# A residual convolution: the first image pair is stored from ACT's queue, beside the last loads of SyncE's queue

## Chip, cores, metric

One core of one Trainium2 chip. Times are device microseconds of one execution, as the median of several runs. A "span" is the time from the first to the last instruction in the records of a run; it leaves out a part at the end (1.83 us in the profiled run of the kernel before: 123.0 us against a span of 121.17 us). In the profile lines PE is TensorE (PEld its weight loads), DVE is VectorE, ACT is ScalarE, POOL is GpSimd and SP is SyncE; q1 is the DMA queue that SyncE fills, q10 the one that ACT fills.

## The reference

```python
x:        (16, 64, 64, 64) float32
weight:   (64, 64, 3, 3)   float32
residual: (16, 64, 64, 64) float32
# 3x3 convolution, padding 1, summed over input channels, then
return (output + residual).astype(np.float32)
```

## The kernel before

The images are handled in pairs. A pair of x, of residual or of output is one tile of 128 partitions x 4096 floats, 2.097 MB. SyncE's queue issues all loads and then all stores; only one half of the first x pair comes from ACT's queue. ACT casts x to bf16, TensorE does six accumulating matmul passes per image, VectorE adds the result to the residual in place (tile `ro`), and `ro` is stored.

```python
def load_ro(p):
    nc.sync.dma_start(out=ro[p][:, :], in_=res_bc[128*p : 128*p+128, :]).then_inc(s_r[p], 16)

def store(p):
    return nc.sync.dma_start(out=out_bc[128*p : 128*p+128, :], in_=ro[p][:, :])

# SyncE
for p in range(NPAIR):                       # NPAIR = 8, NXR = 3 buffers for x
    if p >= NXR:
        nc.sync.wait_ge(s_half, 2 * (p - NXR) + 3)
    ...                                      # p == 0: first half of x, and the weights
    else:
        load_x(p)
    load_ro(p)
for p in range(NEARLY):                      # NEARLY = 6
    nc.sync.wait_ge(s_add, 2 * p + 3)
    store(p).then_inc(s_out, 16)

# ACT
for n in range(B):                           # 16 images
    if im == 0:
        nc.scalar.wait_ge(s_x[p % NXR], ...)
    ... two casts ...

# after all engines have met
for p in range(NEARLY, NPAIR):
    store(p)                                 # SyncE, the last two pairs
```

## Time and profile before

| | before |
|---|---|
| time, median of the first 3 runs | 123.16 us (123.14 to 123.23) |
| bytes moved | 50.48 MB |
| last addition ends | 104.1 us |
| last store issued | 104.8 us |
| last store landed | 120.2 us |

The page divides the span into 40 slices of 3.03 us. Its row "DMA" is the busy share of the 16 DMA engines in tenths, and the row "GB/s" under it is what they moved. A transfer issued by an engine's sequencer waits in that engine's queue; the row of the sequencer (SPq, ACTq) shows the issue alone, not the movement. The Trainium skill says so too ("Perfetto Trace Analysis", section "DMA Instruction — HWDGE (DVE, Sync)"), and the trace agrees: issues take 0.33 to 0.58 us, and stores land 11 to 35 us later.

### The profile page before, as it was taken

The numbers are of one execution on the slowest core, as the hardware profiler recorded it, in microseconds if no ns is written. First come the engines' busy times: TensorE is split into PE (matmuls) and PEld (weight loads), VectorE is DVE, ScalarE is ACT, GpSimd is POOL, SyncE is SP. The second block draws the span as 40 slices with busy tenths as digits, with TensorE's granted clock in tenths as the row PEclk, the third lists the DMA queues.
The fourth block names the chain that finished last, engine by engine and source line by source line (L and its number), as shares of the span: only waits on it lengthen the run. The fifth ranks groups of instructions, "written<-read, shape, count | busy, mean of one in ns | idle before, by whom it ended". The sixth has DMA issues, their size and how long they took to land.

```text
span 121.2 us, 736 instructions
## 1 busy us (share of the span) xinstructions
PE 87.7 (72%) x389; PEld 10.7 (9%) x105; DVE 76.0 (63%) x40; ACT 63.1 (52%) x37; POOL 2.4 (2%) x16
## 2 busy tenths in 40 slices
PE   0033499999999999999999999999999980000000
PEld 0021001101010101010101010101010100000000
DVE  0005300889898898989889898898989889300000
ACT  4049969938966984993993994896000000000000
POOL 5200000000000000000000000000000000000000
PEclk9999999999999999999999999999999999755555
DMA  6999999999999999999999999999999999999993
GB/s 168 427 444 433 433 433 433 433 427 433 433 427 427 433 433 427 427 433 427 433 433 433 433 433 422 433 389 433 433 433 433 422 433 433 433 433 433 427 433 151
DMA packets 3744, 50.48 MB, mean 417 GB/s; under 512 B 416, under 2 KB 544, under 8 KB 544
## 3 DMA queue, kind: packets, MB, share of 16 engines
q1 hardware_dynamic: 3600, 49.43, 96.3%
q10 hardware_dynamic: 144, 1.05, 2.0%
HBM read 33.70 MB, written 16.78 MB: 417 GB/s over the span
## 4 chain that ended last, share of the span: by engine, by line
PE 71%; DVEq 2%; DVE 2%; issue 0%
PE ps L86 53%; PE ps L85 17%; DVEq L129 2%; DVE ro L201 2%
## 5 line engine op out<-in xcount | busy, mean ns | idle before, releaser
L201 DVE TENSOR_TENSOR ro<-ps,ro 64x2048 f32<-64x2048 f32 x32 | 73.2, 2289 | 17.7 <-PE ps L86 17.2
L86 PE MATMUL ps<-xp,wl 128*128 128x504 bf16 (+1 forms) x288 | 80.0, 388 | 0.2
L173 ACT CAST xp<-xr 64x2048 bf16<-64x2048 f32 x16 | 30.3, 1896 | 19.3 <-DMA xr<-in_x_dram 17.1
L85 PE MATMUL ps<-xp,wl 128*128 128x504 bf16 (+1 forms) x92 | 35.8, 389 | 3.4 <-PEq L222 3.4
L177 ACT CAST xp<-xr 64x2048 bf16<-64x2048 f32 x16 | 30.4, 1897 | 0.4
L85 PEld LDWEIGHTS ps<-xp,wl 128*128 128x128 bf16 x96 | 9.5, 99 | 79.1 <-issue 79.1
L189 DVE CAST wl<-ps 32x192 bf16<-32x192 f32 x8 | 2.8, 348 | 10.4 <-PE ps L214 10.3
L214 PE MATMUL ps<-ident,wraw 128*32 128x128 f32 x9 | 2.1, 412 | 8.1 <-DMA wraw<-in_weight_dram 8.1
L214 PEld LDWEIGHTS ps<-ident,wraw 128*32 128x32 f32 x9 | 1.2, 137 | 8.6 <-issue 8.1
L173 ACT ACT_TABLE_LOAD x1 | 1.3, 1283 | 1.1 <-SPq L129 1.1
L182 ACT CAST wl<-ps 32x192 bf16<-32x192 f32 x4 | 1.2, 306 | 0.0
L160 POOL MEMSET xp<- 64x64 bf16 x4 | 0.6, 147 | 0.2
L159 POOL MEMSET xp<- 64x64 bf16 x4 | 0.6, 145 | 0.2
L148 POOL TENSOR_SCALAR_AFFINE_SELECT ident<-ident 128x128 f32<-128x128 f32 x1 | 0.3, 295 | 0.2 <-POOL ident L146 0.2
L162 POOL MEMSET wl<- 64x192 bf16 x1 | 0.3, 253 | 0.1
L161 POOL MEMSET wl<- 64x192 bf16 x1 | 0.3, 252 | 0.1
L146 POOL MEMSET ident<- 128x128 f32 x1 | 0.2, 205 | 0.7 <-SPq L129 0.7
L257 POOL MEMSET const-uint8-127<- 128x1 uint8 x1 | 0.1, 113 | 0.0
L257 POOL MEMSET const-bfloat16-1.0<- 128x1 bf16 x1 | 0.1, 112 | 0.0
L257 POOL MEMSET const-float32-1.0<- 128x1 f32 x1 | 0.1, 109 | 0.0
L257 POOL MEMSET const-float32-0.0<- 128x1 f32 x1 | 0.1, 104 | 0.2 <-issue 0.2
## 6 DMA issues: line engine op xcount, KB each, us to landing
ro<-in_residual_dram SPq DMA_DIRECT2D x8, 2048.0 KB, 21.9
out_dram<-ro SPq DMA_DIRECT2D x8, 2048.0 KB, 28.2
xr<-in_x_dram SPq DMA_DIRECT2D x7, 2048.0 KB, 17.5
xr<-in_x_dram SPq DMA_DIRECT2D x1, 1024.0 KB, 7.0
xr<-in_x_dram ACTq DMA_DIRECT2D x1, 1024.0 KB, 7.6
wraw<-in_weight_dram SPq DMA_DIRECT2D x1, 144.0 KB, 6.9
```

Of the source, the lines that this page charges most:

```text
L85: return e.matmul(out=out_, lhsT=lhsT, rhs=rhs, start=start, stop=stop, skip_group_check=True)
L86: return e.add_instruction(mybir.InstMatmult(name=nc.get_next_instruction_name(), engine=PE, ins=[e.lower_ap(rhs), e.lower_ap(lhsT)], outs ...
L129: with tc.tile_critical(no_gpsimd_drain=True):
L159: nc.gpsimd.memset(t[0:64, 0, :], 0.0).then_inc(s_id, 1)
L160: nc.gpsimd.memset(t[64:128, J, :], 0.0).then_inc(s_id, 1)
L173: i = nc.scalar.copy(out=t[64:128, 0:J, :], in_=x4[hp, :, 0, :])
L177: nc.scalar.copy(out=t[0:64, 1 : J + 1, :], in_=x4[hp, :, 1, :]).then_inc(s_pack, 1)
L182: i = nc.scalar.copy(**weight_block(h, *b))
L189: i = nc.vector.tensor_copy(**weight_block(h, *b))
L201: i = nc.vector.tensor_tensor(out=o4[hp, :, par, :], in0=psj[64 * par : 64 * par + 64, :, :], in1=o4[hp, :, par, :], op=ADD)
L214: i = nc.tensor.transpose(out=tp[0:32, t // 3, 128 * (t % 3) : 128 * (t % 3) + 128], in_=wraw3[:, :, t], identity=ident[:, :])
L257: nc = _bacc.Bacc("TRN2", target_bir_lowering=False, num_devices=1)
```

## The change

The intent: store 0 should no longer wait for all loads to be through SyncE's queue. ACT issues it while the last loads are under way.

```diff
-    def store(p):
-        return nc.sync.dma_start(out=out_bc[128 * p : 128 * p + 128, :], in_=ro[p][:, :])
+    def store(p, engine=nc.sync):
+        return engine.dma_start(out=out_bc[128 * p : 128 * p + 128, :], in_=ro[p][:, :])
...
-        for p in range(NEARLY):
+        for p in range(1, NEARLY):
             nc.sync.wait_ge(s_add, 2 * p + 3)
             store(p).then_inc(s_out, 16)
... in ACT's loop over the images, after the casts:
+            if n == 12:
+                nc.scalar.wait_ge(s_add, 3)
+                store(0, nc.scalar).then_inc(s_out, 16)
```

## The prediction

> **What bounds the kernel now.** First the page, for which resource is busy in every slice.
>
> ```profile
> PE   0033499999999999999999999999999980000000
> ...
> DMA  6999999999999999999999999999999999999993
> ...
> DMA packets 3744, 50.48 MB, mean 417 GB/s; under 512 B 416, under 2 KB 544, under 8 KB 544
> ...
> q1 hardware_dynamic: 3600, 49.43, 96.3%
> q10 hardware_dynamic: 144, 1.05, 2.0%
> ```
>
> The DMA row has a 9 in 38 of its 40 slices, while PE begins in the third slice and is done seven slices (21 us) before the end. SyncE's queue q1 and ACT's queue q10 together hold the 16 DMA engines for 98.3% of the span. The chain of waits gives PE 71%, but it follows the compute to 104.1 us and does not account for the stores that drain after it, so I don't take it for the bound. The bound is 50.48 MB through engines that are never idle.
>
> Second, the DMA view of a stretch with loads alone (44 to 76 us) and of one with stores alone (84 to 116 us):
>
> ```profile
> DMA packets 957, 13.84 MB, mean 433 GB/s; under 512 B 112, under 2 KB 112, under 8 KB 112
> ```
> ```profile
> DMA packets 956, 13.83 MB, mean 432 GB/s; under 512 B 112, under 2 KB 112, under 8 KB 112
> ```
>
> Both directions run at the same rate to 0.3%. A pair of images is 128 x 4096 x 4 B = 2.097 MB, so one pair-sized transfer takes 2.097 MB / 433 GB/s = 4.84 us.
>
> Third, the border between loads and stores, in windows one slice wide (the last two columns are the DMA share and GB/s):
>
> ```profile
> 75.75:78.78 3.03, 3.03 (x15) 0.39 (x4) 2.42 (x3) 2.50 (x2) 0.00 (x0) 1.00 1.09 427
> 78.78:81.81 3.03, 3.03 (x16) 0.30 (x4) 3.00 (x2) 3.00 (x2) 0.00 (x0) 1.00 0.95 395
> 81.81:84.84 3.03, 3.03 (x16) 0.39 (x4) 2.46 (x2) 2.09 (x2) 0.00 (x0) 1.00 1.00 427
> ```
>
> The border costs (433 - 395) / 433 x 3.03 us = 0.27 us. That is all there is to win at it.
>
> Fourth, the timeline of ACT, for when the moved store is issued and how long ACT can be late:
>
> ```profile
> 68.45 1.90 ACT L177 CAST xp<-xr 64x2048 bf16<-64x2048 f32 x1
> 70.37 1.90 ACT L173 CAST xp<-xr 64x2048 bf16<-64x2048 f32 x1
> 72.29 1.90 ACT L177 CAST xp<-xr 64x2048 bf16<-64x2048 f32 x1
> 76.26 1.90 ACT L173 CAST xp<-xr 64x2048 bf16<-64x2048 f32 x1 [2.08 <-DMA xr<-in_x_dram]
> ```
>
> The casts of image 12 end at 70.35 us; the last x load (pair 7) has landed at 76.2 us. From the tile views of residual and output, by issue and landing: the last residual load, issued at 59.1 us, lands 22.2 us later (81.3); store 0, issued at 59.6, lands 26.6 later (86.2); store 5, issued at 86.3, lands 24.2 later (110.5); stores 6 and 7 are issued at 104.4 and 104.8 and land at 115.3 and 120.2. Spaced 4.9 us apart, they leave no hole.
>
> **What the Trainium skill says.** The page "DMA: Bandwidth & Descriptors", section "Issuing engines are not separate DMA queues", says that transfers from different issuing engines "will ultimately run on the same 16 DMA engines and interleave" and that spreading them saves only sequencer time. The trace agrees as far as it can: in the second and third slices, where the halves of the first x pair were in flight from SyncE and ACT, the page has 427 and 444 GB/s, the same as with one queue. Its section "Queues, rings and completion order" has each engine take turns between its queues, one packet at a time. No stretch of this trace has a load and a store in flight from two queues, so what alternating directions cost is not shown. Its section "Where 436 GB/s comes from" gives 435 GB/s as the ceiling of the SBUF ports; the measured 433 and 432 are at it.
>
> **The change part by part.**
> 1. Removed from SyncE: one wait and one issue (0.38 us median in the tile view of the output). The wait for the first pair's additions (over at about 34.4 us, when the first addition of image 2 ends) has long been satisfied at 59.6 us, and SyncE then waits for VectorE anyway (24.9 us in four waits before store issues). Gain: 0.
> 2. Added on ACT: one issue after image 12's casts, some 0.4 us. ACT idles 2.08 us before image 14, so it costs 0.
> 3. Moved: 2.097 MB, from behind the last residual load to beside the last two loads. Bytes and engines stay: 0 by itself.
> 4. The loads are held up. The first slice moved 168 GB/s x 3.03 us, 1.18 us' worth at full rate, so data began about 1.85 us after the first issue. By that estimate store 0 starts at about 72.2 us. The last x load has run since 71.4 (76.2 - 4.84) and has 4.0 us of work left; at half the engines' time it lands at 80.2. Store 0 then has 0.8 us of work left, shared with the last residual load: done near 82. The residual load lands near 86.1 and store 1 follows where it began before.
> 5. Can the delay reach the end? Image 14 is cast from 80.2 to 84.1 instead of from 76.3, image 15 by 87.9. VectorE starts images at 94.33 and 99.52 us, so an image takes PE 5.19 us, and PE begins image 14 at about 89.1 and image 15 at 94.3: 5.0 and 6.4 us of slack. Even with store 0 served entirely first (4.84 us of delay) 4.1 us remain. The last residual is needed at 94.3, over 8 us after it lands. Behind that lies a second slack: store 6 is issued at 104.4, and its data could start only when store 5 is through at 110.5; minus 1.85 us of start, 4.2 us.
> 6. The border. One border becomes a mixed stretch of about 10 us and a clean load-to-store border (residual to store 1). Between a gain of 0.27 us, if mixing covers it, and some tenths lost in the alternation. I take +0.05.
>
> Sum: 123.16 + 0 + 0 + 0 + 0.05 = 123.2 us.
>
> **The rivals.**
> *Both directions at once are faster.* If a load and a store used different halves of some path, the 4.84 us of store 0 would be hidden, whole or in part: at most 123.16 - 4.84 = 118.3 us. For it: this trace has no mixed stretch that rules it out. Against it: the engines are already at a share of 1.0 with one direction, and loads and stores run at one rate, as if set by the engines and not by the direction. Covering the border alone would give 122.9.
> *Alternating is slower.* A transfer has 128 rows, 8 on each engine, so alternating row by row makes about 16 turns on each. If each cost what the one turn costs now, 16 x 0.27 = 4.3 us: 127.5 us. For it: the turn is visible. Against it: with two queues ready an engine has work of the other to go on with, and 0.27 us probably belongs to the end of the last load rather than to each change of direction. A tenth of that, 0.4 us, is easily possible.
> *The late x load becomes the bound.* ACT, PE and VectorE would finish later and store 6 would come late. It takes more than 4.1 + 4.2 us of delay; the largest I can construct is 4.84. Then 123.2 still.
>
> **Range and chances.** Repeats of the kernel before lie within 0.1 us, so the range is that of the mixing: 122.6 (border covered, slight overlap) to 124.0 (some tenths of turn costs). Faster by 2% means below 120.7, half of store 0 hidden: 0.02. Slower by 2% means over 125.6, most of the turn cost real: 0.05. Within 2%: 0.93.
>
> **What would show each step.** Q10 carries 3.15 MB instead of 1.05, in 288 packets, the total stays 50.48 MB. ACT's idle time before image 14 grows from about 2 us to about 6, and that cast starts near 80.2 us. PE and VectorE keep their times, the last addition ends near 104.1. The DMA row stays at 9, with 433 GB/s in the mixed stretch (72 to 82 us); well above means the first rival, well below the second. Store 1 lands near 91 as before, store 7 near 120.2. The prediction is wrong if the mixed stretch leaves the 420 to 445 GB/s band, or if the stores after it no longer follow each other 4.9 us apart.

## The result

The changed kernel took 123.34 us (123.25 to 123.61, 6 runs), against 123.15 us (123.01 to 123.23, 6 runs). The ratio is 1.002, with a 95% interval of 1.0008 to 1.0033: the same at 2%, and a small loss beyond the scatter. A ratio here is the mean time of one kernel's fast runs over that of the other's of the same rounds, so not quite the ratio of the medians.

The page of the changed kernel:

```profile
PE   0033599999999999999999999999999950000000
...
DMA  6999999999999999999999999999999999999993
GB/s 173 426 448 431 431 431 431 431 426 437 426 431 431 431 431 431 431 431 431 426 437 426 388 388 431 431 431 431 431 431 431 431 431 426 431 431 431 426 431 146
DMA packets 3744, 50.48 MB, mean 415 GB/s; under 512 B 416, under 2 KB 544, under 8 KB 544
...
q1 hardware_dynamic: 3456, 47.33, 92.2%
q10 hardware_dynamic: 288, 3.15, 6.1%
```

Same bytes and same packets, with 2.10 MB moved from q1 to q10. What is new are the two neighbouring slices of 388 GB/s, the 23rd and 24th (66.8 to 72.9 us).

The two low slices, and the border between the last residual load and store 1 at about 86 us, in windows of the changed kernel (start:end, length, busy time of PE, PEld, DVE, ACT, POOL, granted clock, DMA share, GB/s):

```profile
66.66:69.69 3.03, 2.98 (x15) 0.34 (x4) 2.45 (x2) 3.00 (x2) 0.00 (x0) 1.00 1.08 400
69.69:72.72 3.03, 3.03 (x16) 0.29 (x3) 2.78 (x2) 2.98 (x3) 0.00 (x0) 1.00 0.95 373
...
81.81:84.84 3.03, 3.03 (x16) 0.37 (x4) 2.45 (x2) 3.01 (x2) 0.00 (x0) 1.00 1.01 433
84.84:87.87 3.03, 3.03 (x16) 0.32 (x4) 3.00 (x2) 2.98 (x3) 0.00 (x0) 1.00 1.01 433
```

And the stretch between them, in one window:

```profile
72.00:82.00 10.00, 10.00 (x48) 1.07 (x11) 8.78 (x5) 2.29 (x3) 0.00 (x0) 1.00 1.01 433
```

Three readings. The ten microseconds in which loads and the store share the engines run at 433 GB/s, exactly as loads alone did. The border at about 86 us, where store 1 follows the last residual load, shows no dip at all. All of the loss is where the store enters: (433 - 400 + 433 - 373) / 433 x 3.03 us = 0.65 us, against 0.27 us at the border of before (its windows stand in the prediction).

The single packets of the trace show which transfers pay. A row of a pair is one packet of 16,384 bytes, and in each of these traces the median of such packets is 611 ns. In the changed kernel 43 of them that begin between 68.21 and 70.69 us took over 625 ns, up to 1121. All 43 are on q1, which then carries loads alone; their extra time is 0.69 us on each of the 16 engines in the mean. So the loads that are under way slow down, from 1.8 us after the store's issue until its own packets begin, and no packet of the store is slow. This is the view of 68.2 to 70.2 us (packets of q1 alone, at 303 GB/s, and yet the engines are counted as 97.7% busy):

```profile
DMA packets 37, 0.61 MB, mean 303 GB/s; under 512 B 0, under 2 KB 0, under 8 KB 0
...
q1 hardware_dynamic: 37, 0.61, 97.7%
```

The border of before looks the same: 28 packets between 77.67 and 79.58 us, before the last residual load landed (80.7 us at the earliest), with 0.36 us of extra time on each engine. Why the loads slow down is not shown.

ACT's timeline in the changed kernel:

```profile
66.36 1.90 ACT L173 CAST xp<-xr 64x2048 bf16<-64x2048 f32 x1 [2.08 <-DMA xr<-in_x_dram]
66.41 0.36 ACTq L79 DMA_DIRECT2D out_dram<-ro  x1
68.28 1.90 ACT L177 CAST xp<-xr 64x2048 bf16<-64x2048 f32 x1
70.20 1.90 ACT L173 CAST xp<-xr 64x2048 bf16<-64x2048 f32 x1
72.12 1.90 ACT L177 CAST xp<-xr 64x2048 bf16<-64x2048 f32 x1
81.71 1.90 ACT L173 CAST xp<-xr 64x2048 bf16<-64x2048 f32 x1 [7.69 <-DMA xr<-in_x_dram]
```

The store stands after image 12's two casts in the program, but it was issued at 66.41 us, while the first of them had just begun. ACT's sequencer runs ahead of the casts. The store's first packet is recorded at 70.28 us. The last x load lands late, so the cast of image 14 begins at 81.71 instead of 76.26 us. VectorE does not notice; its last two images even start 0.5 us earlier than before (94.33 and 99.52 us):

```profile
93.83 4.61 DVE L205 TENSOR_TENSOR ro<-ps,ro 64x2048 f32<-64x2048 f32 x2 [0.58 <-PE ps L86]
99.01 4.61 DVE L205 TENSOR_TENSOR ro<-ps,ro 64x2048 f32<-64x2048 f32 x2 [0.58 <-PE ps L86]
```

One row of the page misleads. It gives ACT's store a median of 34.7 us from issue to landing. All the early stores count on one semaphore, and the landing is matched in order of issue; the fourth group of 16 increments, at 101.1 us, is put down to a store that was the fourth issued. The trace's completion records show the first group complete at 81.1 us, right after ACT's last packet with data (ended at 80.1 us). That is store 0.

### The profile page after: what moved, and what is told of

Read it like the earlier page. It is cut to its first block, busy times and chain, and to the rows that moved or that the text cites. A ratio compares the mean times of both kernels' runs of the same rounds, so it can differ in the third digit from the quotient of the medians.

```text
span 121.5 us, 736 instructions
## 1 busy us (share of the span) xinstructions
PE 87.3 (72%) x389; PEld 10.7 (9%) x105; DVE 76.0 (63%) x40; ACT 63.1 (52%) x37; POOL 2.4 (2%) x16
## 4 chain that ended last, share of the span: by engine, by line
PE 70%; DVEq 2%; DVE 2%; issue 0%
PE ps L86 53%; PE ps L85 17%; DVEq L129 2%; DVE ro L205 2%
## 6 DMA issues: line engine op xcount, KB each, us to landing
out_dram<-ro ACTq DMA_DIRECT2D x1, 2048.0 KB, 34.7
```

## The experiments

All were run in five rounds beside the kernel before. The theories are named as the expectations name them. Two measures are used besides the time: dips in GB/s where a store enters, and the moments at which each of the 16 DMA engines completes its part of a transfer, from the trace's completion records (each transfer leaves 16 of them, one from each engine; they do not say which engine).

### Where and how the store enters

**The early store in SyncE's own queue**, twice (the repeat because the first profile fell on one of the fastest runs):

```diff
+            if p == NPAIR - 1:
+                nc.sync.wait_ge(s_add, 3)
+                store(0).then_inc(s_out, 16)
             load_ro(p)
-        for p in range(NEARLY):
+        for p in range(1, NEARLY):
```

> Store 0 goes into SyncE's own queue between the last x load and the last residual load: it is early as in the changed kernel, but no two queues share the engines. Theory A (the first store of the run pays once, wherever it stands, and pays about double when it enters beside loads from a second queue): one dip of about 0.3 us near 74 us, none between the last residual load and store 1, time that of before, 123.15 +- 0.1. Theory B (every change from load to store pays 0.3 us, alternating or not): two dips, 123.4 or more. Theory C (only sharing between two queues pays the extra): time of before, but it says nothing on where the dips are.

> The kernel with store 0 in SyncE's queue between the last x and the last residual load once more, because its first profile fell on its fastest runs (121.3 of 121.3 to 121.7 us) and its two dips summed to no more than the one of before. Theory B': span 121.5 to 121.6 in the median, two dips that together lose 0.3 us more than the border of before. If the median comes out at that of before, 121.2, the first result was scatter.

Measured: 123.38 us (ratio 1.0029, 1.0013 to 1.0044), then 123.52 us (1.0022, 1.001 to 1.0034). The median span of the second was 121.7 us, against 121.3 for before. So no second queue is needed for the loss: theories A and C, which both expected the time of before, fall. The profile of the second run, at the entry of the store and at the border to store 1:

```profile
72.90:75.90 3.00, 3.00 (x15) 0.29 (x3) 2.97 (x2) 1.17 (x1) 0.00 (x0) 1.00 1.01 393
81.10:84.10 3.00, 3.00 (x15) 0.39 (x4) 2.42 (x2) 2.98 (x2) 0.00 (x0) 1.00 1.01 431
84.10:87.10 3.00, 3.00 (x15) 0.29 (x3) 2.97 (x2) 0.29 (x1) 0.00 (x0) 1.00 1.02 431
```

One dip, (431 - 393) / 431 x 3.00 = 0.26 us, no more than before had at its border, and nothing like it later (the next window, 87.1 to 90.1 us, has 421): the dips of theory A, but not its time. Theory B' (theory B kept to one queue: each change from load to store costs 0.2 to 0.3 us), which wanted two, fails on this profile, though its span came out as expected. (The first profile had 405 and 410 GB/s in two slices; that run was one of the two fastest of its six.) The mean rate therefore does not explain a span 0.4 us longer. What does is in the completion records: the moment at which each engine finished store 7, counted from the first of the 16.

```text
before        0 .03 .03 .06 .06 .11 .15 .16 .19 .21 .33 .34 .35 .39 .45  .55
changed       0 .01 .03 .07 .12 .14 .15 .25 .25 .28 .31 .35 .41 .45 .46  .63
SyncE, early  0 .01 .04 .08 .08 .12 .14 .19 .23 .24 .26 .35 .36 .44 .50 1.20   (repeat)
```

One engine of the 16 is 0.7 us behind the next. It was behind already when the last residual load completed (1.14 us after the first engine), and every transfer after that keeps the lag. The kernel ends with the last engine.

**The same ACT store six images earlier, and two stores one behind the other:**

```diff
-            if n == 12:
+            if n == 6:
```
```diff
             if n == 12:
-                nc.scalar.wait_ge(s_add, 3)
-                store(0, nc.scalar).then_inc(s_out, 16)
+                for q in range(2):
+                    nc.scalar.wait_ge(s_add, 2 * q + 3)
+                    store(q, nc.scalar).then_inc(s_out, 16)
```

> The changed kernel with its ACT store six images earlier (after image 6's casts instead of image 12's), in the middle of the loads. Theory A: one dip of about 0.6 us near 38 to 42 us, none where loads end and store 1 begins, 123.35 as in the changed kernel. Theory B: the dip at the early mix and again 0.3 us at the border near 86 us, 123.6. A third theory (the changed kernel loses because it delays the last loads of the chain) expects the loss to go, 123.15.

> Stores 0 and 1 both from ACT, one behind the other, so the stretch with a load and a store in turn on every engine is about twice as long (some 20 us). Theory A: the loss is paid once at its start, 123.35 as in the changed kernel, mixed stretch at 430 to 433 GB/s after its first 3 us. Theory C (turns between load rows and store rows pay in proportion to their number): twice the extra, about 123.55, and a lower rate all through the mixed stretch.

Measured: 123.50 us (1.0034, 1.0019 to 1.0048) and 123.53 us (1.0039, 1.0025 to 1.0053). The GB/s rows of the two pages:

```profile
GB/s 167 423 450 431 441 431 431 431 431 431 431 431 431 318 436 436 436 431 431 431 431 431 431 431 431 431 431 431 431 431 431 431 431 431 431 431 431 431 431 129
```
```profile
GB/s 178 428 450 431 431 431 431 431 431 431 431 431 436 431 431 431 431 431 431 431 436 431 377 383 431 431 431 431 431 431 431 431 431 431 426 431 431 431 431 124
```

In each there is one dip, where ACT's first store enters: 318 in the early one (41 us; (431 - 318) / 431 x 3.04 us = 0.80 us), 377 and 383 in the other (0.72 us). Where the loads end and SyncE's first store begins, there is none. With two ACT stores the shared stretch is twice as long (ACT's last packet ends at 90.7 us) and stays at 431. So turns between store rows and load rows cost nothing once they run. The early entry was also meant to test whether the loss comes from delaying the last loads. It cannot decide that: every load behind the store moves back, and the last x load landed as late (81.9 us) as in the changed kernel (81.6; before 76.2). The packets decide it: in the changed kernel the slow ones are over at 70.7 us, before a late load has kept anything waiting, and the last addition then ends earlier than before. By their ratios the two kernels lie 0.14 and 0.19% above the changed one, but in other rounds.

**Two separate entries from ACT** (store 0 after image 6, store 1 after image 12), and the changed kernel once more in the same rounds:

```diff
-            if n == 12:
-                nc.scalar.wait_ge(s_add, 3)
-                store(0, nc.scalar).then_inc(s_out, 16)
+            if n in (6, 12):
+                q = n // 6 - 1
+                nc.scalar.wait_ge(s_add, 2 * q + 3)
+                store(q, nc.scalar).then_inc(s_out, 16)
```

> Stores 0 and 1 from ACT, but in two separate entries (after image 6's and image 12's casts), ACT's queue empty between them. If each entry of a store beside loads pays: two dips of about 0.65 us (near 40 and 69 us), none near 86 to 91 us, about 0.65 us above the changed kernel of the same rounds. If the first store of the run pays once: one dip near 40 us, the time of the changed kernel.

> The changed kernel unaltered, for a comparison in the same rounds: 0.2% above before (123.2 to 123.5), dip of about 0.6 us near 69 us, none near 86 us. If it comes out at 0.35%, the early entry and the two ACT stores of the earlier call cost no more than the change itself; if at 0.2%, they cost some 0.15 us more.

Measured: 124.21 us (1.0091, 1.0074 to 1.0108), and 123.41 us for the changed kernel (1.002, 1.0001 to 1.004; single runs from 122.95 to 123.90, so the size of its loss differs from run to run). By its ratio of 1.002 the repeat falls on the branch in which the early entry and the two stores cost some 0.15 us more; the intervals overlap, so this stays open. For the two stores that much lies after the span (time minus span 1.95 to 2.03 us, instead of 1.83). Store 1 was issued at 72.69 us. Windows of the kernel with two entries, around the first entry, the second, and the wait for the late x load:

```profile
39.00:42.00 3.00, 3.00 (x15) 0.34 (x4) 2.66 (x2) 2.95 (x3) 0.00 (x0) 1.00 0.97 273
...
72.00:75.00 3.00, 3.00 (x16) 0.39 (x4) 2.42 (x2) 2.33 (x2) 0.00 (x0) 1.00 1.02 437
75.00:78.00 3.00, 3.00 (x16) 0.29 (x3) 2.96 (x2) 2.98 (x2) 0.00 (x0) 1.00 1.02 437
...
87.00:90.00 3.00, 1.91 (x9) 0.10 (x1) 2.42 (x2) 2.81 (x2) 0.00 (x0) 1.00 0.99 426
90.00:93.00 3.00, 1.87 (x9) 0.29 (x3) 2.97 (x2) 2.95 (x3) 0.00 (x0) 1.00 1.00 426
```

The second entry has no dip, and no slow packet either: here the first store from ACT alone pays. PE stalls at 87 to 93 us (1.91 and 1.87 us busy of 3.00) because the last x load, now delayed twice, completed only at 87.1 us. The last addition ended at 106.3 us, 2.2 us later than in before, and yet the median span rose by only 0.6 us, from 121.2 to 121.8. Compute can be late at the end without the stores running dry.

The time rose by more than the span. It lies 0.8 us above the changed kernel of the same rounds, near the 0.65 us of the branch in which each entry pays, but the span (121.8 against 121.55) lies only 0.25 us above. Time minus span is 2.4 to 2.6 us here, instead of 1.83. The trace has one packet of 8192 bytes at 124.4 us, after the last instruction, on a third queue that is neither SyncE's nor ACT's and that carries instructions (the other kernels use it only before the span, the one with the early entry also 0.1 us into it). The same appears once more below.

### Is it the second queue, or the store?

**A load, not a store, from ACT in the middle of SyncE's loads; and store 0 from ACT, but only after the last load has landed:**

```diff
+            if n == 10:
+                load_ro(6, nc.scalar)          # and not from SyncE
```
```diff
-            if n == 12:
+            if n == B - 1:
+                nc.scalar.wait_ge(s_r[NPAIR - 1], 16)
                 nc.scalar.wait_ge(s_add, 3)
```

> The kernel before, with one residual load (pair 6) issued from ACT's queue in the middle of SyncE's loads; all stores as before. Theory D: a dip of about 0.65 us where the ACT load enters (near 58 us), and the border dip of before as well, 123.7. Theory E: no dip at the entry, 430 GB/s throughout, the border dip alone, 123.1.

> Store 0 again from ACT's queue, but only once the last residual load has landed, so it enters beside stores and not beside loads. Theory D (a second queue that starts on busy engines costs some 0.65 us whatever the two carry): the dip of before (about 0.3 us) at the border near 80 us and another of about 0.65 us near 83 us, 123.6 to 123.8. Theory E (the loss belongs to stores that enter load traffic, and is larger from a second queue): the border dip alone, time of before, 123.1.

Measured, the load: 123.09 us (0.9998, 0.9982 to 1.0015). It was issued at 56.74 us; its first packet is recorded at 60.19 us:

```profile
57.00:60.00 3.00, 3.00 (x16) 0.39 (x4) 2.39 (x3) 2.98 (x2) 0.00 (x0) 1.00 1.01 431
60.00:63.00 3.00, 3.00 (x15) 0.29 (x3) 2.42 (x2) 2.95 (x3) 0.00 (x0) 1.00 1.00 426
...
78.00:81.00 3.00, 3.00 (x16) 0.39 (x4) 2.63 (x2) 2.95 (x3) 0.00 (x0) 1.00 1.02 404
```

No dip where a load enters from the second queue, and the border of before in its place. Theory D falls.

Measured, the late store: 123.53 us (1.0033, 1.0011 to 1.0054), which looks like theory D. But its median span is 121.2 us, that of before in the same rounds; the difference is wholly in what follows the span (2.0 to 2.5 us instead of 1.83), and its trace too has one 8192-byte packet after the end, at 123.3 us. Its GB/s row has the border's dip alone (422 and 406) and nothing near 84.8 us, where ACT's first packet starts. So theory E stands on the spans: a store that joins stores costs nothing while the program runs. The extra 0.6 us after the end of both profiled runs goes with such a late packet, which no other profile has; that the packet causes it was not tested, and the two stores from ACT, with 0.1 to 0.2 us extra, have none.

### Does the size of the early store matter?

**128 KB instead of 2 MB:** the first 1 KB of each row of store 0 goes early, once from SyncE's queue (pair 5), once from ACT's (image 12). The rest is stored behind the loads. The edit is shown for SyncE's queue, cut; for ACT's the added store stands where the changed kernel has it.

```diff
+                store(0, slice(0, 256)).then_inc(s_out, 16)             # SyncE, p == 5
...
-            store(p).then_inc(s_out, 16)
+            store(p, slice(256 if p == 0 else 0, NPIX)).then_inc(s_out, 16)
```

> The kernel before, with the first 1 KB of each row of store 0 (128 KB) stored early from SyncE's queue, between the x and the residual load of pair 5; store 0 then carries the rest, so the bytes stay the same. Theory A: the dip of about 0.3 us goes with the small store to about 54 us, and the border near 81 us has none (427 to 433 GB/s in all windows there); time of before, 123.15 to 123.3. Theory B: the border near 81 us keeps its dip, and the small store brings its own, 123.4. If the dip depends on how many bytes are queued as stores, the small one shows nothing and the border keeps its own: 123.15.

> The small store (first 1 KB of each row of pair 0, 128 KB) from ACT's queue after image 12's casts, among the loads; the rest of store 0 behind the loads in SyncE's queue. If it is the entry of a store from the second queue that costs, whatever its size: a dip of 0.6 us near 68 us, none at the border near 81 us, 123.4. If the cost goes with how many rows of stores and loads share the engines in the first microseconds: a trace of a dip near 68 us, the border near 81 us keeps its 0.2 to 0.3 us, time of before, 123.0 to 123.1.

Measured: 122.94 us (0.9989, 0.9975 to 1.0003) and 123.01 us (0.9984, 0.9971 to 0.9996). The ACT version at its entry and at the border:

```profile
66.00:69.00 3.00, 2.95 (x15) 0.32 (x4) 2.42 (x2) 2.42 (x2) 0.00 (x0) 1.00 1.01 431
69.00:72.00 3.00, 3.00 (x16) 0.36 (x4) 2.97 (x2) 2.98 (x2) 0.00 (x0) 1.00 1.07 453
...
78.00:81.00 3.00, 3.00 (x15) 0.29 (x3) 2.42 (x2) 2.95 (x3) 0.00 (x0) 1.00 1.03 400
```

The small store costs nothing, and it does not spare the border its dip. So it is not "the first store of the run" as such (theory A in its first wording): a small first store neither pays nor pays for the others. Of both expectations the branch held in which the cost goes with the amount stored. Both small-store kernels lie nominally 0.1 to 0.2% below before, near the edge of their intervals; a gain of that size is not one to rely on.

### Does it repeat in one queue?

**Two full stores among the loads, both in SyncE's queue** (with pairs 5 and 7):

```diff
+            if p in (5, 7):
+                q = (p - 5) // 2
+                nc.sync.wait_ge(s_add, 2 * q + 3)
+                store(q).then_inc(s_out, 16)
             load_ro(p)
-        for p in range(NEARLY):
+        for p in range(2, NEARLY):
```

> No store on ACT; store 0 in SyncE's queue between the x and residual load of pair 5, store 1 between those of pair 7: three changes from load to store in one queue, two back to loads. Theory B' (in one queue each change from load to store costs 0.2 to 0.3 us): three dips, span about 0.5 us above before, 123.6. Theory G (the first full store among loads costs once, some 0.3 to 0.4 us over before, whichever queue carries it, as the single early store in SyncE's queue did): 123.4, one large dip near 57 us, little at the later changes.

Measured: 123.84 us (1.0053, 1.0039 to 1.0067), median span 122.0 us against 121.3. The dips look like theory G (386 in two slices near 55 us, 418 in one near 90 us, none at the middle change), the time like theory B'. Neither is right, and the completion records say why:

```text
finish of store 7, us after the first engine
0 .14 .14 .16 .16 .19 .25 .27 .33 .36 .44 .57 .62 .62 1.09 1.48
```

Two engines straggle. From 27 to 52 us the 16 engines were 0.44 to 0.47 us apart. At the x load directly ahead of the first early store they were 1.13 apart, so the lag begins in the loads before the store, as the slow packets do; at the load behind it 1.08, after the last residual load 1.50. A mean over 16 engines hardly shows two stragglers, but the end waits for them. The engines' moments, from the landing of the x load of pair 3 (near 37 us, before any store enters) to store 7, one profiled run each:

| kernel | mean of 16, us | last to last, us | spread at store 7, us |
|---|---|---|---|
| before | 83.04 | 82.98 | 0.55 |
| load from ACT | 82.88 | 83.20 | 0.96 |
| ACT store after the loads | 82.92 | 82.92 | 0.62 |
| small store, SyncE / ACT | 82.98 / 83.02 | 83.12 / 83.11 | 0.64 / 0.76 |
| early in SyncE's queue, two runs | 83.07 / 82.97 | 83.34 / 83.62 | 0.89 / 1.20 |
| two early in SyncE's queue | 83.33 | 84.15 | 1.48 |
| changed, two runs | 83.35 / 83.59 | 83.49 / 83.76 | 0.63 / 0.92 |
| ACT: early / two together | 83.39 / 83.34 | 83.57 / 83.61 | 0.87 / 0.80 |
| ACT: two entries | 83.79 | 83.90 | 1.01 |

A full store that enters load traffic from ACT puts the engines back by 0.3 to 0.75 us in the mean (first column). One early store in SyncE's own queue leaves the mean where it was and puts one or a few engines back (last column; in its first profile six or seven of the 16 engines lagged, in the repeat one). Both raise the second column, which is what the clock sees. The row of the load from ACT warns how far one profile goes: its last engine is 0.2 us later than before's with no difference in the time.

The extra time of the slow packets, on each engine in the mean, sorts the kernels in the same way. At the entry of a full store from ACT it is 0.67 to 1.08 us in five profiles. It is at most 0.01 us at the entry of the load, of the store after the loads and of the small store; these three kernels keep 0.22 to 0.29 us at the border.

## Why the prediction was right or wrong

The time and the class were right: 123.2 was said, 123.34 measured, within 122.6 to 124.0. That the number is close is in part luck: step 6 missed a loss of 0.65 us and a gain of 0.27 us, which offset each other in part. By its steps:

- **The bound (right).** DMA is busy in the same 38 slices, with the same bytes. The compute moved and the end did not follow it: the last addition ends at 103.6 instead of 104.1 us, and the span is 0.35 us longer.
- **Steps 1 and 2, issue costs (right).** The issue on ACT took 0.36 us, hidden.
- **Step 4, the delay of the loads (right in kind, its inputs wrong).** I let the store be issued after image 12's casts at 70.35 and start 1.85 us later, at 72.2. It was issued at 66.41 and started at 70.28, 3.9 us after its issue. The 1.85 us came from idle engines at the start; for the first packet on busy ones it is not valid. (The loads did begin to slow down 1.8 us after the issue.) The cast of image 14 began at 81.71, not near 80.2, and ACT's idle time before it grew to 7.69 us, not to about 6.
- **Step 5, slack (right, with less of it).** "Even with store 0 served entirely first (4.84 us of delay)" was meant as the largest delay. Measured from cast to cast it was 81.71 - 76.26 = 5.45 us, about what store 0 and the entry's own loss make together (4.84 + 0.65). VectorE starts image 14 at 93.83, so PE begins it at 93.83 - 5.19 = 88.6 us, and image 14's second cast ends at 85.5: 3.1 us of slack were left. The second slack, behind the first, was real: with two entries the compute ended 2.2 us late, and the span gave up only 0.6.
- **Step 6, the border (the term that was mis-sized).** I expected a border of 0.27 us to stay between the last residual load and store 1, and the mixed stretch to add +0.05 net. In fact that border vanished (433 GB/s), and the entry of the store lost 0.65 us in its place. Net in the profile: 0.65 - 0.27 = 0.38 us, beside 0.35 us of span; in the medians, +0.19 us.
- **First rival, both directions at once faster:** refuted, 433 GB/s over 72 to 82 us.
- **Second rival, turns cost:** refuted in its form. About 16 turns on each engine cost nothing measurable; what cost was the entry.
- **Third rival, the late x load:** never bound in the changed kernel.

What is shown: the loss comes with a full-sized store entering load traffic. It is paid by the loads under way, in the 2 to 3 us before the store's own packets take over. It does not come from sharing by itself (a load from ACT costs nothing), from the later loads being late (the slow packets come before), or from the number of turns. What stays open: why these loads slow down at all, why a second entry from ACT does not pay again, why the change from loads to stores is free after a store came in from ACT but not after a small one, and why in one queue it hits single engines and from two queues all of them.

## What to carry to other kernels

In this kernel, whose DMA engines are busy from start to end, reordering transfers moved landing times and left the sum, but for a few tenths. In one like it, ask what the new order costs where it begins, and whether what lands later has slack. Compare how long packets of one size take, before and during a dip: it tells which transfers pay. Look at the last of the 16 engines and not only at the mean rate: a kernel that ends with a store ends with the engine that lags. And before a difference of half a microsecond is explained by the trace, compare the spans, since some of it may lie after the last instruction.

## What the Trainium skill lacked or had wrong

- "DMA: Bandwidth & Descriptors", section "Issuing engines are not separate DMA queues": holds for the bandwidth (433 GB/s mixed, 433 alone). It lacks that a full-sized store put in among loads costs something: mean delay of the engines 0.3 to 0.75 us when it came from ACT's queue, 0.0 us in the mean but up to 0.7 us on one engine when it was placed early in SyncE's. The loads pay it: in the changed kernel packets of 16,384 bytes took up to 1121 ns, instead of 611, just before the store's own began.
- The same page, section "Why a DMA increments its semaphore by 16 and not by 1": says that the engines of one transfer finish independently, as here, but has no number for how far they drift apart in a long run: 0.55 us in before, 1.48 us with two stores among the loads of one queue, where the lag of 1.50 us at the last load was kept to the end.
- The same page, section "Latency and other measured facts", gives about 600 ns to the first byte of a transfer from SyncE or ACT. At the start of before, SyncE's first packet came 1.0 us after its issue began and 0.6 us after the issue ended. On busy engines the first packet came 3.9 us after the issue (66.41 to 70.28 us; a store), and 3.4 us for the load from ACT (56.74 to 60.19 us).
- No page has the extra time after the last instruction that two of the kernels showed (time minus span 2.0 to 2.6 instead of 1.83 us), together with one 8192-byte packet on the instruction queue after the end of the span.
